# A hybrid RWKV-7 / HGRN-2 step on one core: value tiles turned in 32x32 blocks by VectorE and put in place by the stores

## The chip, the cores and the metric

The kernel runs on one core of one Trainium2 chip. The time is device microseconds of one launch. The kernel before took 1773.77 us (median of 3 runs, 1771.31 to 1775.47). PE is TensorE, PEld its weight load, DVE VectorE, ACT ScalarE, POOL GpSimd and SP SyncE, whose queue only issues transfers.

## The reference

One layer of a diffusion backbone, all in float32, over 1024 latent tokens and 128 context tokens (T = 1152). Cut to what matters here:

```python
u = h @ w_in                                   # h = modulated rmsnorm(x), [T, 1024]
q, i, zf, zb, g = split(u[:, :2560], 5)        # HGRN-2: 4 heads x 128; i are its inputs (values)
o_a = hgrn2_scan(silu(q), 1 - f, heads(i), log f) in both directions, rmsnorm, * silu(g)
r, k, v, ... = split(dwconv1d(u[:, 2560:]))    # RWKV-7: 8 heads x 64; v are its values
S = S * w_t - (S kk)(kk a) + v_t k_t;  y_t = S r_t          # in both directions
bonus = sum(r * k * r_k) * v
x = x + gate1 * (concat(o_a, o_b) @ w_out)
x = x + gate2 * ((gelu(dwconv2d(h2 @ w_gate) + b) * (h2 @ w_up)) @ w_down)
```

The projections of `w_in` come out with channels on partitions and tokens along the free axis. Two of the results are needed the other way round, tokens on partitions: the RWKV-7 values `v` (the recurrence and the bonus read them by token) and the HGRN-2 inputs `i` (right-hand side of the products over tokens).

## The kernel before

The program runs in these stages, which overlap: modulation and norm of the input; projections of `w_in` (768 groups of three fp32r matmuls of 128x128 by 384 columns, L1070 to L1072, from a high and a low part of each operand) with the RWKV-7 features of four channel pairs (`features`, from L1309) and a 32x32 elimination per pair (`elim`); the RWKV-7 recurrence (`chains`, 18 steps of 64 tokens in two groups of heads), interleaved with the HGRN-2 blocks (`hgrn_block`, `hgrn_out`); the output projection; the feed-forward part (22 blocks of channels, L2065, seven products of a Strassen-like scheme); and its down projection (L2229).

What is turned. For each pair `p` and block `tb` of 384 tokens, `features` takes `v[:, c]` [128 channels, 384 tokens] for the forward direction and a reversed copy `vs` (by POOL or ACT, L1349) for the backward one. TensorE turns each in three 128x128 transposes against `ident` into PSUM (L1353), ACT or DVE copies the result to `vt` (L1355, two buffers), and one or two transfers store it in the DRAM tensor `d_v` (`vx`), tokens as rows, in pieces of 128 floats (L1359). `hgrn_in` does the same for the part "i" of each head: copy out of PSUM (L1234), three transposes (L1238), copy (L1239), one store to `d_hv` (L1240), which holds [128, 9, 128]: for each partition the nine 128-token tiles in a row. `d_v` is loaded by `load_values` (L1703) into `X`, which POOL or ACT copies once more (L1704), and by `bonus_rows`; `d_hv` by `hgrn_block` (L1550) and `hgrn_out` (L1650).

What sets the order. The program is first recorded as some 9,600 operations. Three tables then fix everything: `SEQUENCE` is the order in which operations are issued, and so the order of each engine's own instructions; `ENGINE_OF` has a letter (V, A, G, S for DVE, ACT, POOL, SP) for each operation that could go to more than one engine, among them all copies written with `copy` and all stores written with `st` (POOL or SP); `PLACE_OF` names the buffer of each tile. Each engine works strictly in its own order and waits where an operand isn't there. Nothing is decided at run time.

Of the kernel before, what the change touches and what calls it, by code (L numbers as in the profile page):

```python
# [493 lines left out]
class Plan:  # L494


    HELPERS = ("mm", "st", "copy", "combine", "split", "load_w", "record", "either", "acc", "fetch")
    ENGINES = ("PE", "DVE", "ACT", "POOL", "SP")
    LETTER = {"V": "DVE", "A": "ACT", "G": "POOL", "S": "SP"}
    BITS = 23  # L500
# [1899 lines left out]
```

## Time and profile before

| | us |
|---|---|
| median of 3 runs | 1773.77 |
| profiled execution, whole | 1778.03 |
| its span, first to last instruction | 1776.3 |
| PE busy | 1711.1 |
| DVE busy | 1424.9 |
| ACT busy | 949.4 |
| POOL busy (transfers that it issues not counted) | 354.6 |

The span in stages, from the profile's stretches: start 0 to 44 us; projections and features to about 488 us; recurrence and HGRN-2 blocks to about 933 us; output projection to 1037 us; feed-forward part to about 1520 us; down projection to the end. How to read it: "busy" on PE includes the time in which small matmuls drain, so 96% is not peak arithmetic, but it is the share of the span in which TensorE was not waiting. A row of a group gives operation, output and input names, shape and count, then busy us and mean ns of one, then the idle time just before it and who ended that.

### The profile page before, as it was taken

How to read it: one execution, taken by the hardware profiler on the slowest of the kernel's cores; microseconds unless marked ns; L12 is line 12 of the kernel's file. 1: busy time of each engine (PE TensorE's matmuls, PEld its weight loads, DVE VectorE, ACT ScalarE, POOL GpSimd, SP SyncE). 2: the span in 40 equal slices, each digit the busy share in tenths (PEclk: the TensorE clock that was granted, in tenths of full speed). 3: DMA queues.
4: the chain of work that ended last, by engine and by line, in shares of the span. 5: the costliest groups of instructions: out<-in, count | busy, mean ns of one | idle time of the engine just before them, and what ended most of it. 6: DMA issues, size and time to landing. Idle time of an engine off the chain costs nothing.

```text
span 1776.3 us, 44618 instructions
## 1 busy us (share of the span) xinstructions
PE 1711.1 (96%) x17726; PEld 1544.9 (87%) x17726; DVE 1424.9 (80%) x2722; ACT 949.4 (53%) x1977; POOL 354.6 (20%) x546
## 2 busy tenths in 40 slices
PE   6999999999999989999999999999999999999998
PEld 4888888889988888887877889999999999888886
DVE  6548988988787878786767888898888888979765
ACT  6655766662266655564645664444444444665542
POOL 2003133153311011112210013323333322000000
PEclk8999999999999999999989999999999999999999
DMA  9326456486676678889987657877877777898683
GB/s 308 98 86 163 109 136 154 120 227 208 183 225 196 203 214 277 275 279 265 312 245 271 224 120 146 176 152 160 170 156 153 158 158 157 274 316 275 196 273 130
DMA packets 341838, 352.97 MB, mean 199 GB/s; under 512 B 69817, under 2 KB 264398, under 8 KB 341278
## 3 DMA queue, kind: packets, MB, share of 16 engines
q1 hardware_dynamic: 287518, 284.85, 52.9%
q0 software_dynamic: 54112, 65.27, 19.2%
q8 instruction: 139, 2.28, 0.5%
q14 instruction: 69, 0.57, 0.1%
HBM read 254.99 MB, written 118.10 MB: 210 GB/s over the span
## 4 chain that ended last, share of the span: by engine, by line
PE 73%; DVE 4%; DMA 4%; ACT 3%; issue 1%; POOL 1%; SPq 0%; DVEq 0%; ACTq 0%; POOLq 0%
PE banks L2065 27%; PE banks L2229 14%; PE banks L1070 4%; PE banks L1072 4%; PE banks L1071 4%; PE banks L1713 2%; PE banks L1955 1%; PE banks L1957 1%; PE banks L1956 1%; PE banks L1582 1%; PE banks L1784 1%; PE banks L1627 1%; PE banks L1760 1%; PE banks L1767 1%; PE banks L1786 1%
## 5 line engine op out<-in xcount | busy, mean ns | idle before, releaser
L1070 PE MATMUL banks<-hh,wh 128*128 128x384 f32 x768 | 278.2, 362 | 0.6 <-DVE fx L1250 0.6
L1072 PE MATMUL banks<-hh,wl 128*128 128x384 f32 x768 | 258.7, 337 | 0.0
L1071 PE MATMUL banks<-hl,wh 128*128 128x384 f32 x768 | 258.4, 336 | 0.0
L2153 DVE SCALAR_TENSOR_TENSOR low<-low,pf 128x1024 f32<-128x1024 f32 x176 | 225.7, 1282 | 10.6 <-ACT low L2147 8.0
L2065 PE MATMUL banks<-qm,wh 128*128 128x320 f32 x968 | 223.4, 310 | 0.2 <-ACT wh L2035 0.2
L2065 PE MATMUL banks<-hbm,wh 128*128 128x256 f32 x880 | 162.9, 282 | 1.5 <-ACT low L1935 1.5
L2065 PE MATMUL banks<-qm,wl 128*128 128x320 f32 x528 | 162.8, 308 | 0.2 <-DVE wl L2035 0.2
L2065 PEld LDWEIGHTS banks<-qm,wh 128*128 128x128 f32 x968 | 161.0, 189 | 0.6 <-ACT wh L2035 0.5
L1070 PEld LDWEIGHTS banks<-hh,wh 128*128 128x128 f32 x768 | 144.8, 188 | 15.7 <-issue 9.3
L1071 PEld LDWEIGHTS banks<-hl,wh 128*128 128x128 f32 x768 | 145.2, 189 | 2.7 <-issue 1.2
L1072 PEld LDWEIGHTS banks<-hh,wl 128*128 128x128 f32 x768 | 144.9, 189 | 0.0
L2065 PEld LDWEIGHTS banks<-hbm,wh 128*128 128x128 f32 x880 | 139.3, 190 | 1.8 <-ACT low L1935 1.7
L2065 PE MATMUL banks<-ham,wh 128*128 128x256 f32 (+1 forms) x616 | 131.7, 294 | 0.0
L2065 PE MATMUL banks<-hbm,wl 128*128 128x256 f32 x440 | 124.4, 283 | 0.0
L2102 ACT COPY fx<-banks 128x256 f32<-128x256 f32 (+1 forms) x132 | 52.0, 397 | 110.2 <-PE banks L2065 98.2
L2065 PEld LDWEIGHTS banks<-ham,wh 128*128 128x128 f32 x616 | 101.4, 190 | 0.3
L2065 PEld LDWEIGHTS banks<-qm,wl 128*128 128x128 f32 x528 | 99.1, 188 | 0.4 <-DVE wl L2035 0.4
L2035 ACT CAST wh<-low 128x512 fp32r<-128x512 f32 x82 | 50.5, 618 | 69.4 <-PE banks L2065 60.5
L2065 PEld LDWEIGHTS banks<-hbm,wl 128*128 128x128 f32 x440 | 84.0, 191 | 0.0
L2065 PE MATMUL banks<-ham,wl 128*128 128x256 f32 (+1 forms) x264 | 77.0, 292 | 0.0
L2035 DVE TENSOR_TENSOR wl<-low,wh 128x512 fp32r<-128x512 f32 x82 | 56.2, 689 | 22.8 <-ACT wh L2035 20.7
L2035 ACT CAST wh<-wr 128x512 fp32r<-128x512 f32 x72 | 44.6, 622 | 54.3 <-PE banks L2065 43.8
(586 smaller groups left out, 4368.2 us busy)
## 6 DMA issues: line engine op xcount, KB each, us to landing
wr<-in_w_in_dram SPq DMA_DIRECT2D x34, 512.0 KB
d_t<-in_ffn_w_down_dram POOLq DMA_DIRECT2D x60, 256.0 KB, 6.5
low<-d_a SPq DMA_DIRECT2D x54, 256.0 KB
low<-d_ak SPq DMA_DIRECT2D x64, 192.0 KB
low<-d_kb SPq DMA_DIRECT2D x36, 256.0 KB
d_a<-low POOLq DMA_DIRECT2D x16, 576.0 KB, 4.7
top<-in_ada_w_dram SPq DMA_DIRECT2D x17, 512.0 KB
low<-in_ada_w_dram SPq DMA_DIRECT2D x32, 256.0 KB
```

The source lines that it names most:

```text
L1070: mm(o, wh[:, kt, :], hh[:, kt, c], kt == 0, False)
L1071: mm(o, wh[:, kt, :], hl[:, kt, c], False, False)
L1072: mm(o, wl[:, kt, :], hh[:, kt, c], False, kt == KT - 1)
L1582: mm(pv[r, i, :], xs[:, t0:t0 + 32], view(qy, t0, [[2 * m, 16 // m], [B + m, 2], [1, m]]), True, True)
L1627: mm(ps[:, i * P:(i + 1) * P], kt[:, i * P:(i + 1) * P], val[:, i, :], True, True)
L1713: mm(pa[h][:, P * w:P * w + P], kb[hc[h], w, :], W[hc[h], A0[h] + 192 * w:A0[h] + 192 * w + P], True, True)
L1760: mm(R[hc[h], 64 * w:64 * w + 64], av(h, w, 0), X[h][:, 0, w], True, True)
L2035: split(*w, src)
L2065: pe.matmul(o, a[:, kt, :], b[:, kt, :], start=start and first, stop=last, skip_group_check=not start)
L2102: act.copy(keep[n], y[:, 0:w])
L2153: dve.scalar_tensor_tensor(av, shifted(dy, dx), tap(3 * dy + dx), av, MUL, ADD)
L2229: pe.matmul(o, x, y, start=fresh and f, stop=l, skip_group_check=not fresh)
```

## The change

The value tiles are no longer turned by TensorE. A DVE transpose turns each 32x32 block of the [128, 384] tile within its place: partition 32a + i, column 32b + j becomes partition 32a + j, column 32b + i. Partition quadrant `a` then still holds channels 32a to 32a + 31, now along the columns of each block, and tokens of the block on partitions. The new `turned_store` sends four transfers, one per quadrant, which put the block of 32 tokens and 32 channels at its rows and columns; a piece is 32 floats, 128 bytes. `d_hv` becomes [T, 128], tokens as rows, so its two loads take three pieces of 512 bytes per partition where they took one of 1536 bytes. The copy out of PSUM in `hgrn_in` is ACT's alone now. PSUM tiles and their second copies go away.

```diff
-    hvd = [dram(f"d_hv{h}", [P, NT, P]) for h in range(4)]
+    hvd = [dram(f"d_hv{h}", [T, P]) for h in range(4)]
...
-                    copy(ta, ps)
-                    pv = pbank()
-                    with plan.together():
-                        for j in range(3):
-                            pe.transpose(pv[:, j * P:(j + 1) * P], ta[:, j * P:(j + 1) * P], ident)
-                    copy(tb_, pv[:, 0:384])
-                    st(hvd[h][:, 3 * tb:3 * tb + 3, :], tb_.rearrange("p (a b) -> p a b", b=P))
+                    act.copy(ta, ps)
+                    dve.transpose(tb_, ta)
+                    turned_store(hvd[h][tb * 384:(tb + 1) * 384], tb_, 0)
...
+    def turned_store(rows, blocks, at):
+
+        n = rows.shape[0] // 32
+        for a in range(4):
+            st(rows[:, 32 * a:32 * a + 32].rearrange("(b i) c -> i b c", i=32),
+               blocks[32 * a:32 * a + 32, 32 * at:32 * (at + n)].rearrange("p (b c) -> p b c", c=32))
 ...
-                ps = pbank("sp")
-                with plan.together():
-                    for j in range(3):
-                        pe.transpose(ps[:, j * P:(j + 1) * P], vs[:, j * P:(j + 1) * P], ident)
                 vt = tl("vt", [P, 384])
-                copy(vt, ps[:, 0:384])
+                dve.transpose(vt, vs)
                 for ch, n0, n in steps_of(d, 6 * (2 - tb if d else tb), 6):
-                    at = (ch - 6 * (2 - tb if d else tb)) // 2
+                    at = 2 * (ch - 6 * (2 - tb if d else tb))
                     w0 = P * (2 * (p % 2) + d)
-                    st(vx[p // 2][64 * n0:64 * (n0 + n), w0:w0 + P].rearrange("(a p) c -> p a c", p=P),
-                       vt.rearrange("p (a b) -> p a b", b=P)[:, at:at + n // 2, :])
+                    turned_store(vx[p // 2][64 * n0:64 * (n0 + n), w0:w0 + P], vt, at)
 ...
-        ld(val, hvd[h][:, 3 * tb:3 * tb + 3, :])
+        ld(val, hvd[h][c].rearrange("(a p) e -> p a e", p=P))
 ...
 SEQUENCE = [int(i) for i in """
-1 2 17 6 18 19 0 12 13 14 15 7 11 177 184 10 27 28 4 3 20 21 29 30 33 22 24 16 34 26 31 32
+228 229 11 1 0 12 13 14 27 8 17 18 2 28 19 4 3 15 29 30 20 21 31 16 33 39 22 24 25 32 81 26
```

The three tables are new as a whole, so the order moves on every engine, also where the code is the same. In counts: 108 matmuls fewer on PE, 36 STREAM_TRANSPOSE more on DVE, 18 + 11 copies fewer on ACT; the transfers that store `d_v` go from 32 to 128, those of `d_hv` from 12 to 48; POOL issues 487 transfers in place of 357, SP 1187 in place of 1185. Of the 72 copies of values in the recurrence POOL now has 40 for 45, and of those of L1769 DVE has 6 for 15. TensorE's order keeps its large shape: the projections, features and steps of the recurrence stand at nearly the same counts of each other.

TensorE in the first block of values (L1343 is the bonus product and L1364 the decay projections; in the new program the lines are L1350 and L1366, and the projections L1074 to L1076). Before:

```order
L1072 MATMUL banks<-hh,wl_136 128x384
L1343 MATMUL banks<-hsum,top 128x2 x3
L1353 MATMUL banks<-c_ident,low 128x128 x3
L1353 MATMUL banks<-c_ident,top 128x128 x3
L1070 MATMUL banks<-hh,wh_133 128x384
```

Now:

```order
L1076 MATMUL banks<-hh,wl_136 128x384
L1350 MATMUL banks<-hsum,top 128x2 x3
L1074 MATMUL banks<-hh,wh_134 128x384
L1075 MATMUL banks<-hl,wh_134 128x384
L1076 MATMUL banks<-hh,wl_136 128x384
```

The six transposes of the two directions are gone, and projections follow at once.

DVE at the same place in the new program (L1283 the convolution's taps, L1268 the low part of a weight, L1331 to L1343 the first features; in brackets what a row waits for):

```order
L1283 SCALAR_TENSOR_TENSOR low<-low,pt 128x1024
L1358 STREAM_TRANSPOSE top<-low 128x384 [waits DVE_49]
L1358 STREAM_TRANSPOSE top<-top 128x384 [waits Activation_49]
L1268 TENSOR_TENSOR wl_136<-wr,wh_134 128x1024 [waits DMAHW3_49,PE_49,Activation_49]
L1358 STREAM_TRANSPOSE top<-low 128x384 [waits DMAHW6_49,DMASW3_49,DMAHW7_49,DMASW2_49,DVE_49]
L1358 STREAM_TRANSPOSE top<-top 128x384 [waits DMAHW1_49,DMAHW0_49,DMAHW5_49,DMASW4_49,Pool_49]
L1331 SCALAR_TENSOR_TENSOR top<-low,pt,top 128x1152 [waits Activation_49]
```

Before, no transpose of values stood on DVE. The third and fourth wait for the four transfers each of the first and second (DMAHW are SP's, DMASW POOL's), because `vt` has two buffers. The first features stand behind them.

POOL at the start of the recurrence (L1704, now L1706, the copy of values; L1820, now L1822, a store of outputs; L1798, now L1800, the decay of the state; L1613, now L1615, a small copy of the HGRN-2 blocks). Before:

```order
L1704 COPY low<-low 64x256 [waits DMAHW1_49,PE_49]
L1704 COPY low<-low 64x256 [waits DMAHW6_49,Pool_49]
L1704 COPY low<-low 64x256 [waits DMAHW2_49,PE_49]
L1613 COPY gres<-top 128x2x3 [waits DVE_49,Pool_49]
L1820 DMA d_y<-top 128x256 [waits DMASW5_49,Activation_49]
L1798 TENSOR_TENSOR low<-low,dcs 128x256 [waits DVE_49]
L1704 COPY low<-low 64x256 [waits DMAHW3_49,PE_49,Pool_49]
```

Now:

```order
L1706 COPY low<-low 64x256 [waits DMAHW5_49,PE_49]
L1800 TENSOR_TENSOR top<-top,dcs 128x256 [waits DVE_49,Pool_49]
L1800 TENSOR_TENSOR low<-low,dcs 128x256 [waits DVE_49,Activation_49]
L1822 DMA d_y<-top 128x256 [waits DMASW7_49,Activation_49]
L1615 COPY gres<-top 128x2x3 [waits DVE_49]
L1633 DMA d_hu_111<-fx 128x384 [waits DMASW0_49]
L1706 COPY low<-low 64x256 [waits DMAHW3_49,PE_49,Pool_49]
L1822 DMA d_y<-top 128x256 [waits DMASW1_49,Activation_49]
L1248 DMA d_hf_98<-fx 128x384 [waits DMASW2_49,Activation_49]
L1706 COPY low<-low 64x256 [waits DMAHW5_49,PE_49]
```

More stores stand between the copies: 103 transfers between POOL's first and last copy of values, where there were 44; SP's list between its first and last load of values is 551 rows long, where it was 603.

More of the change, by code (lines that the diff above doesn't have):

```diff
@@ new lines @@
+    "VAVAVVVAVVAAAAAAAAVVVVVASSSSGSSSSGGGGGSSGSGVVAVAVAAAAAAVVAAVVVAAVVVAVAAVAVVVAVAAGASASVSVSASVSAGVSVVGSSSASSGGVVAAGGGGVAAAGSSGAASSGSGSSSSVVAVSGSSVAAAGSG"
+    "GAASSSGSGGSGSSGSGSGSAAAAAAVSGSSSGSSVAAAAAASGGSGGGSSSSASAGASAAAAAAAASGGSSGSGGGGSSSGGSGGGSSGGAAGSSSAGSGSAAAVSGGSAAAAGGSSVASGSSASSGGVAAVSSSGAAAASSGSVASSS"
+    "SGSSGASGGGGGSSVAAAAAASGSGSSSSVAVAAAASGSGSGSSGSSASAGASAAAAAAAVGSSSGGSSGSSGGGSSSSGSGGSSAASSSSGGSSSVAAAGSGSAAAVGSGSAAGGSSGSGSGAAAASSSSVAVASSGGVAGSSSSSGSA"
+    "SGGGSSGSVAAAAAASGGSSSGSVAAAAVASGGGGGGGSGSGSGAAAAAAAASGGGSSGSGSGSSGGGSGGSSSSSAASGGSAGSSSAVAAGGSGAAAAGSGSVAGSGSGSSGGVAAASSSSAAAASSSGVAGGSSGGGSAGSGGGGSSA"
@@ L494 @@
 class Plan:
-    HELPERS = ("mm", "st", "copy", "combine", "split", "load_w", "record", "either", "acc", "fetch")
+    HELPERS = ("mm", "st", "copy", "combine", "split", "load_w", "record", "either", "turned_store", "acc", "fetch")
     ENGINES = ("PE", "DVE", "ACT", "POOL", "SP")
@@ L1649, in hgrn_out @@
             ld(sc, hsd[h][:, 3 * tb:3 * tb + 3, :])
-            ld(val, hvd[h][:, 3 * tb:3 * tb + 3, :])
+            ld(val, hvd[h][c].rearrange("(a p) e -> p a e", p=P))
             ld(g2, hqg[h][:, c])
```

51 lines of the change are left out of this document (24 added, 27 removed), and 603 rows, old and new, of the table SEQUENCE.

## The prediction

> **What bounds the kernel now.** I read the page first (busy shares and slices), then busy time by stretch, the waits of TensorE, and the groups and the chain at the lines that the change touches.
>
> ```profile
> PE 1711.1 (96%) x17726; PEld 1544.9 (87%) x17726; DVE 1424.9 (80%) x2722; ACT 949.4 (53%) x1977; POOL 354.6 (20%) x546
> PE   6999999999999989999999999999999999999998
> ...
> 0.00:44.00 44.00, 30.39 (x220) 20.92 (x220) 28.40 (x85) 30.29 (x63) 9.52 (x29) 0.88 0.94 307
> ...
> 89.00:488.00 399.00, 393.30 (x4270) 354.34 (x4269) 323.27 (x653) 223.93 (x452) 115.18 (x214) 1.00 0.58 154
> 488.00:933.00 445.00, 411.91 (x7636) 360.68 (x7636) 345.54 (x833) 253.97 (x592) 74.19 (x135) 0.98 0.83 249
> ...
> 1300.00:1500.00 200.00, 200.00 (x1504) 200.00 (x1504) 173.27 (x253) 88.24 (x171) 62.17 (x64) 1.00 0.76 154
> ```
>
> In the stretch rows the numbers are the length, then busy time of PE, weight load, DVE, ACT and POOL, the clock, the DMA share and GB/s. TensorE sets the time: it stands 65 us in 1776.3, of which 13.6 us are the loading at the start (DMA share 0.94), 5.7 lie in 89 to 488 us (projections and RWKV features), 33.1 in 488 to 933 (the recurrence), none in 1300 to 1500 (the feed-forward part). Before 488 us, work taken off TensorE should come off the span almost one for one. The 33 us are spread thinly:
>
> ```profile
> PE banks L1713 <- DMA low<-d_ak: 5.8, 4, 2.5
> PE banks L1767 <- ACT low L1762: 3.2, 3, 1.6
> PE banks L1775 <- DVE top L1611: 2.5, 1, 2.5
> ...
> PE banks L1238 <- ACT fx L1234: 1.1, 2, 0.6
> ```
>
> (us in total, times, longest.)
>
> **The change, part by part.** *Removed from TensorE:* 108 transposes, 72 at L1353 and 36 at L1238.
>
> ```profile
> L1238 PE MATMUL banks<-c_ident,fx 128*128 128x128 f32 x36 | 6.6, 291 | 1.1 <-ACT fx L1234 1.1
> L1353 PE MATMUL banks<-c_ident,low 128*128 128x128 f32 x36 | 6.3, 284 | 0.0
> L1353 PE MATMUL banks<-c_ident,top 128*128 128x128 f32 x36 | 6.2, 282 | 0.0
> ...
> 266.02 0.87 PE banks L1353 x6
> 343.48 0.80 PE banks L1353 x6
> ...
> 123.54 0.53 PE L1353 MATMUL banks<-c_ident,low 128*128 128x128 f32 x3
> 123.94 0.55 PE L1353 MATMUL banks<-c_ident,top 128*128 128x128 f32 x3
> 124.24 0.42 PE L1070 MATMUL banks<-hh,wh 128*128 128x384 f32 x1
> ```
>
> Busy time says 6.6 + 6.3 + 6.2 = 19.1 us, the upper end, since overlapping ends are counted. The chain rows give 0.80 to 0.87 us for six, the timeline 0.70 us from the first of six to the next projection matmul (124.24 - 123.54): 108 x 0.117 = 12.6 us is the lower end. I take the larger chain row, 0.87 / 6 = 0.145 us each, because a switch of operand also costs the neighbour something: 15.7 us, 10.4 of it at L1353 and 5.2 at L1238. The wait of 1.1 us at L1238 goes with them. In the order, 99 of the 108 stand ahead of the recurrence, where TensorE is 98.6% busy.
>
> *Moved between ACT and DVE:* of the copies out of PSUM, 18 + 11 go from ACT (481 to 487 ns) and 6 + 1 from DVE; 36 block transposes come to DVE.
>
> ```profile
> L1355 ACT COPY top<-banks 128x384 f32<-128x384 f32 x18 | 8.4, 487 | 2.4 <-PE banks L1353 2.4
> L1355 DVE COPY top<-banks 128x384 f32<-128x384 f32 x6 | 3.3, 556 | 1.3 <-PE banks L1353 1.3
> L1769 DVE COPY low<-banks 64x256 f32<-64x256 f32 x15 | 6.3, 421 | 7.2 <-PE banks L1767 3.5 <-PE banks L1760 1.9 <-ACT low L1769 1.2
> L1436 DVE STREAM_TRANSPOSE top<-low 128x1024 f32<-128x1024 f32 x5 | 6.2, 1239 | 0.0
> L1447 DVE STREAM_TRANSPOSE top<-top 128x1024 f32<-128x1024 f32 x5 | 10.3, 2066 | 0.1
> ...
> 123.00:412.00 289.00, 283.87 (x3303) 251.43 (x3302) 252.38 (x520) 183.27 (x380) 90.92 (x171) 0.99 0.60 153
> ```
>
> No 128x384 block transpose is in the trace. From the contiguous 128x1024 one, 1239 x 0.375 = 465 ns; from the strided one, 2066 x 0.375 = 775 ns. The new ones are contiguous, so I take 0.50 us (the lower figure and a little for the start): 18 us on DVE, bounds 16.7 and 27.9. Against it go 7 copies (3.9 us) and, by the new table of engines, 9 of the 15 copies at L1769 (3.8 us): net 10 us. In the features stretch, 123 to 412 us, DVE goes from 252.4 to about 261 (24 x 0.50 - 3.3) while TensorE goes from 283.9 to 273.5: DVE is then 94% of what TensorE needs. It still fits, but with little room. ACT, 183 of 289 us, only gains.
>
> *Stores.* A tile of values was stored by one or two transfers with pieces of 512 B; now by four per destination with pieces of 128 B.
>
> ```profile
> L1359 SPq DMA_DIRECT2D d_v<-top x22: 360/580/1456, 125.0 to 373.6; - x22
> L1359 POOL DMA_DIRECT2D d_v<-top x10: 563/748/792, 124.9 to 412.1; - x10
> DMA to landing us min/median/max: 2.3/4.4/5.0
> ...
> q1 hardware_dynamic: 12187, 5.26, 45.3%
> ...
> q1 hardware_dynamic: 287518, 284.85, 52.9%
> ```
>
> The first q1 row is of 133 to 178 us, the second of the whole run: 0.453 x 16 x 45 / 12187 = 26.8 ns for packets of 432 B on average, 0.529 x 16 x 1776.3 / 287518 = 52.3 ns for 991 B. A line through both gives 13 ns at 128 B; no saving at all would be 27 ns. 36 tiles x 1536 packets of 128 B take 45 us of all 16 engines (93 at 27 ns) in place of 26 (13,824 packets of 512 B at 30.5 ns). Spread over 123 to 652 us, +19 us (at most +67) against a share of 0.60 stays far from full: cost 0. The value loads in the recurrence get three packets for one, at the same bytes: 24 x 384 x 30.5 / 16 = 18 us of engine time at most in place of part of it; cost 0.
>
> The Trainium skill speaks against these stores: "DMA: Bandwidth & Descriptors", Specifications, puts the minimum transfer for line rate at 512 B, with read-modify-write below. Taken as "128 B costs what 512 B costs", that is the 27 ns above, and the time would move toward the 1768 of rival C, through later landings; the two q1 rows, smaller packets being cheaper, rather contradict it.
>
> The direct cost of the stores is on DVE: `vt` has two buffers, and in the new order the third transpose stands two places behind the first pair, with one weight split between. It waits for four issues (0.58 us on SP, 0.75 on POOL, shared: some 1.5 us) and a landing of up to 5.0 us. DVE stands there some 4 us once; behind it wait `kk` and the first feature products. TensorE has projections queued ahead, so I charge 1 us. The other pairs stand 12 to 50 rows apart.
>
> *The tables.* TensorE's order keeps its shape: at every 48th projection matmul the counts of features, elimination and recurrence matmuls differ by a few. In the recurrence POOL gets 103 transfers between its first and last copy of values, against 44, and SP loses 52 rows. I charge nothing for this, and put it into the rivals.
>
> Sum: -15.7 - 1.1 + 1.0 = -15.8 us, so 1776.3 becomes 1760.5 in the span. The profiled execution took 1778.03 us, 4.3 more than the median of the runs, 1773.77; I carry the difference to the median: **1758 us**.
>
> **Rivals.** *B, more than the transposes:* fewer stores on SP let the loads of the recurrence start earlier, and the new order may close some of the 33.1 us there. For it: 5.8 us of L1713 wait on loads. Against it: the other waits there are many and short. A quarter to half of 33 us: 1742 to 1750.
>
> *C, DVE takes over in the features stretch:* 261 us of work, plus 12 value blocks with some 2 us of waiting for stores each, is 285 of the 289 us. The 10.4 us of L1353 are lost, only the 5.2 at L1238 stay: 1768. Against it: DVE's waits there are now small, and projections buffer TensorE.
>
> *D, slower: POOL's queue in the recurrence.*
>
> ```profile
> L1704 POOL COPY low<-low 64x256 f32<-64x256 f32 x45 | 25.7, 573 | 171.9 <-DMA low<-d_v 129.0 <-PE banks L1582 14.2 <-issue 10.9
> L1820 POOL DMA_DIRECT2D d_y<-top x17 | 9.5, 561 | 54.2 <-ACT top L1817 54.2
> ```
>
> POOL copies the values of each step (40 of 72 now), and every store queued ahead holds that copy by 0.56 us and by whatever the store waits for. 59 more stores x 0.56 = 33 us; if all of it reached the recurrence, 1758 + 33 = 1791. It decides from 48% (15.8 / 33) coming through. For it: POOL is strictly in order, and stores wait for ACT (54.2 us in 12 waits at L1820). Against it: POOL stood 129 us waiting for the loads of values, which these stores can use, and is busy 74 of 445 us.
>
> *E, the change frees TensorE and nothing follows:* the projections only run ahead and the recurrence, bound by its own chain, ends when it did: 1773. Against it: it starts when the work before it is done, 99 transposes sooner.
>
> **How the numbers follow.** The forecast (1750 to 1767) gets 0.48, B 0.20, C 0.15, D 0.13, E 0.04. No change means within 0.2%, 1770.2 to 1777.3. Faster: 0.48 + 0.20 + 0.10 of C = 0.78. Same: 0.05 of C, 0.03 of D, 0.03 of E = 0.11. Slower: the rest, 0.11. The range runs from the low end of B, 1741, to 1778, the part of D that gives back only a little more than the gain; outside lie about 0.03 of B and 0.11 of D.
>
> **What would show it.** Right: TensorE busy about 1692 to 1696 us with some 65 us of standing; 89 to 488 us of today done by about 475, with the first L1713-like matmuls 12 to 15 us earlier; DVE rows of STREAM_TRANSPOSE 128x384 near 0.5 us; the feed-forward part as long as now. C shows as TensorE waiting on DVE products in the features stretch and DVE above 93% there; D as POOL rows of stores ahead of value copies and TensorE waiting for POOL at L1775-like lines; B as less than 25 us of standing in the recurrence. I am wrong if the recurrence or the feed-forward part grows by more than 5 us, or if a transpose on DVE takes 0.78 us.

## The result, and the profile after

The changed kernel takes 1785.64 us (median of 7 runs, 1781.56 to 1794.51), the kernel before on the same chip 1774.65 us (7 runs, 1771.31 to 1778.84): a ratio of 1.0070, 95% interval 1.0047 to 1.0092. It is slower by 0.7%, some 12 us, where 1758 us was forecast. The profiled execution of the changed kernel took 1789.6 us, 4.0 above its median; that of before stood 4.3 above its own, so the two traces can be compared directly. Spans of single executions of one kernel differ by several us, so no difference below some 5 us between two traces is explained here by the traces alone. Medians here and below leave out three slow executions (2329 us of no_turning, 2965 and 5946 us of the kernel before).

The page's busy times after:

```profile
PE 1707.3 (95%) x17618; PEld 1538.5 (86%) x17618; DVE 1441.9 (81%) x2733; ACT 935.5 (52%) x1966; POOL 421.8 (24%) x672
```

All 108 transposes are gone (17726 to 17618), yet PE's busy time fell by 3.8 us only, to 1707.3 where 1692 to 1696 was forecast, and it stands 80.5 us in place of 65.2. Where, is seen when the span is cut at the same points of TensorE's work in both kernels: the first and the 1584th of the 2304 projection matmuls, the first and the last matmul of the gate and up projections (L2065, L2067 after), and the end. Up to the 1584th, the two kernels have the same projection, feature and elimination matmuls; the kernel before has 90 transposes more. Busy time by stretch; columns as in the prediction. Before:

```profile
70.00:454.50 384.50, 378.80 (x4036) 338.41 (x4035) 306.82 (x611) 223.77 (x451) 106.01 (x196) 1.00 0.56 150
454.50:1024.40 569.90, 535.47 (x8501) 467.53 (x8500) 441.52 (x1019) 321.72 (x739) 88.91 (x160) 0.99 0.80 244
1024.40:1535.70 511.30, 508.34 (x3769) 504.54 (x3769) 446.06 (x654) 239.82 (x465) 146.87 (x151) 1.00 0.76 160
1535.70:1776.30 240.60, 232.06 (x1035) 189.30 (x1033) 183.86 (x306) 115.10 (x223) 2.44 (x3) 0.99 0.74 243
```

After:

```profile
72.20:465.40 393.20, 374.75 (x3947) 333.71 (x3947) 319.24 (x637) 211.28 (x434) 144.61 (x265) 0.98 0.59 141
465.40:1031.10 565.70, 534.57 (x8484) 464.99 (x8483) 446.76 (x1020) 321.09 (x744) 124.89 (x231) 0.99 0.82 249
1031.10:1540.30 509.20, 504.27 (x3746) 501.40 (x3745) 444.44 (x648) 235.95 (x460) 141.84 (x142) 1.00 0.75 158
1540.30:1787.80 247.50, 237.90 (x1058) 193.61 (x1057) 187.39 (x311) 118.01 (x228) 3.88 (x5) 0.99 0.74 240
```

The 11.5 us are 2.2 at the start (72.2 against 70.0), 8.7 in the features stretch, -4.2 from there to the end of the recurrence and the output projection, -2.1 in the gate and up projections and 6.9 from there to the end. So the features stretch, from which the gain should have come, is where most was lost. The first L1713 matmul of the recurrence (L1715 after), forecast 12 to 15 us earlier, came 2.5 us later, at 486.3 against 483.8. It isn't at the same place in the two orders: 1728 projection matmuls start before it in the kernel before and 1683 in the changed one, so the new order put 45 of them behind the start of the recurrence: some 8 us of work, estimated from the 0.17 us from one to the next at 344.4 to 345.9 us of the changed kernel. Cut there, the features stretch looks as long as before (414.1 against 413.8 us), but holds less work. That TensorE's order keeps its counts, as is said ahead of the prediction and in it, is right up to the 1584th projection and not at this point.

In the features stretch TensorE's clock was at half for 3.4 us before and for 17.1 us after (the granted clock in the seventh column):

```profile
288.80:292.20 3.40, 3.40 (x49) 2.96 (x52) 3.04 (x6) 2.12 (x5) 0.91 (x2) 0.50 0.60 159
```

```profile
293.50:307.20 13.70, 11.72 (x144) 9.82 (x145) 7.48 (x13) 5.02 (x13) 4.32 (x9) 0.50 0.60 128
413.00:416.40 3.40, 0.71 (x4) 0.39 (x3) 3.33 (x6) 0.49 (x1) 2.36 (x6) 1.00 0.56 187
416.40:419.80 3.40, 3.40 (x12) 3.40 (x12) 3.16 (x10) 0.00 (x0) 3.40 (x7) 0.50 0.96 268
```

Half of the busy time in such pieces is lost: 1.7 us before, (11.72 + 3.40) / 2 = 7.6 after. That gives a balance that is used for the runs below, work at full clock + standing + half clock lost. Up to the 1584th projection it is 377.1 + 5.7 + 1.7 = 384.5 before and 367.2 + 18.4 + 7.6 = 393.2 after: TensorE was spared 9.9 us of work, but stood 12.7 us longer and lost 5.9 us more to the half clock. Up to the first L1713 matmul it is 406.4 + 5.7 + 1.7 = 413.8 before; the runs under the old tables, where TensorE's order is that of before, are compared with this.

What TensorE waited for in 89 to 488 us after, where before no wait was over 1.1 us:

```profile
PE banks L1466 <- issue: 4.1, 2, 3.3
PE banks L1074 <- DVE fx L1250: 2.7, 1, 2.7
PE banks L1399 <- DVE top L1391: 2.3, 1, 2.3
PE banks L1350 <- DVE top L1346: 2.3, 1, 2.3
PE banks L1074 <- ACT low L1275: 1.5, 1, 1.5
PE banks L1074 <- ACT low L1277: 1.5, 1, 1.5
PE banks L1399 <- ACT low L1409: 1.2, 1, 1.2
PE banks L1074 <- ACT low L1279: 1.1, 1, 1.1
```

None of these names a block transpose or a store of values. The transposes themselves, with what DVE waited for ahead of them:

```profile
L1358 DVE STREAM_TRANSPOSE top<-low 128x384 f32<-128x384 f32 x12 | 6.9, 574 | 2.8 <-DMA d_v<-top 2.7
L1358 DVE STREAM_TRANSPOSE top<-top 128x384 f32<-128x384 f32 x12 | 6.9, 572 | 0.5 <-DMA d_v<-top 0.4
L1239 DVE STREAM_TRANSPOSE fx<-fx 128x384 f32<-128x384 f32 x12 | 6.8, 570 | 1.9 <-ACT fx L1238 1.8
```

### The profile page after: what moved, and what is told of

The parts are those of the page before. It is cut to its first block, busy times and chain, and to the rows that moved or that the text cites. A ratio compares the mean times of both kernels' runs of the same rounds, so it can differ in the third digit from the quotient of the medians.

```text
span 1787.8 us, 44540 instructions
## 1 busy us (share of the span) xinstructions
PE 1707.3 (95%) x17618; PEld 1538.5 (86%) x17618; DVE 1441.9 (81%) x2733; ACT 935.5 (52%) x1966; POOL 421.8 (24%) x672
## 5 line engine op out<-in xcount | busy, mean ns | idle before, releaser
L1074 PE MATMUL banks<-hh,wh 128*128 128x384 f32 x768 | 281.1, 366 | 9.1 <-DVE fx L1250 4.8
L1076 PE MATMUL banks<-hh,wl 128*128 128x384 f32 x768 | 260.4, 339 | 0.0
L2067 PE MATMUL banks<-qm,wh 128*128 128x320 f32 x968 | 224.6, 311 | 0.0
L1074 PEld LDWEIGHTS banks<-hh,wh 128*128 128x128 f32 x768 | 146.3, 190 | 29.7 <-issue 10.6
L2067 PE MATMUL banks<-hbm,wh 128*128 128x256 f32 x880 | 162.8, 282 | 2.1 <-ACT fx L2104 2.1
L2067 PE MATMUL banks<-qm,wl 128*128 128x320 f32 x528 | 163.3, 309 | 0.2 <-DVE wl L2037 0.2
L2067 PEld LDWEIGHTS banks<-qm,wh 128*128 128x128 f32 x968 | 161.6, 190 | 0.1
L1076 PEld LDWEIGHTS banks<-hh,wl 128*128 128x128 f32 x768 | 146.0, 190 | 0.0
L2067 PEld LDWEIGHTS banks<-hbm,wh 128*128 128x128 f32 x880 | 139.2, 190 | 2.4 <-ACT fx L2104 2.4
L2067 PE MATMUL banks<-ham,wh 128*128 128x256 f32 (+1 forms) x616 | 132.3, 294 | 0.3 <-DVE ham L1997 0.3
L2067 PE MATMUL banks<-hbm,wl 128*128 128x256 f32 x440 | 124.4, 283 | 0.0
L2067 PEld LDWEIGHTS banks<-ham,wh 128*128 128x128 f32 x616 | 101.6, 189 | 1.0 <-DVE ham L1997 0.5
L2067 PEld LDWEIGHTS banks<-qm,wl 128*128 128x128 f32 x528 | 99.5, 189 | 0.5 <-DVE wl L2037 0.5
L2067 PEld LDWEIGHTS banks<-hbm,wl 128*128 128x128 f32 x440 | 83.9, 191 | 0.0
L2175 POOL DMA_DIRECT2D d_t<-in_ffn_w_down_dram x44 | 50.7, 1254 | 117.1 <-DMA d_t<-d_t 86.7
L2067 PE MATMUL banks<-ham,wl 128*128 128x256 f32 (+1 forms) x264 | 77.0, 292 | 0.0
```

The lines of the kernel that those rows point to most:

```text
L1074: mm(o, wh[:, kt, :], hh[:, kt, c], kt == 0, False)
L1076: mm(o, wl[:, kt, :], hh[:, kt, c], False, kt == KT - 1)
L2067: pe.matmul(o, a[:, kt, :], b[:, kt, :], start=start and first, stop=last, skip_group_check=not start)
L2175: acc(td[j][k], b)
```

## The experiments

The order, the engines and the buffers stand in three tables, so the edit and the tables can be run apart: the old tables were carried over to other code, operation by operation, with new operations put where those that they replace had stood. "Old tables" below means this. The median is of 4 to 12 executions; the ratio is to the kernel before on the same chip (7 to 23 executions, median 1772.9 to 1774.7 us), so the ratios are the safer comparison between rows.

| run | code, tables | us | ratio, 95% interval |
|---|---|---|---|
| changed kernel | changed, new | 1785.6 | 1.0070 (1.0047 to 1.0092) |
| edit_old_tables | changed, old | 1795.6 | 1.0111 (1.0093 to 1.0129) |
| hg_old_tables | HGRN-2 inputs alone, old | 1784.2 | 1.0064 (1.0043 to 1.0086) |
| rw_old_tables | RWKV values alone, old | 1791.9 | 1.0091 (1.0075 to 1.0107) |
| no_turning | no turning, old | 1765.8 | 0.9953 (0.9937 to 0.9969) |
| dve_old_stores | DVE turns, one store, old | 1774.8 | 0.9997 (0.9981 to 1.0014) |
| four_stores | TensorE turns, four stores, old | 1790.2 | 1.0090 (1.0069 to 1.0110) |
| quarter_stores | TensorE turns, four stores of 512 B pieces, old | 1786.2 | 1.0072 (1.0049 to 1.0094) |
| edit_dve_relief | changed, old, 51 operations to ACT | 1806.1 | 1.0174 (1.0150 to 1.0197) |
| edit_spread | changed, old, stores spread | 1809.9 | 1.0216 (1.0190 to 1.0242) |
| edit_pool | changed, old, stores on POOL | 1795.4 | 1.0121 (1.0096 to 1.0147) |
| after_start | changed, new, start loads moved | 1787.5 | 1.0078 (1.0055 to 1.0100) |
| after_old_stores | DVE turns, one store, new | 1783.6 | 1.0052 (1.0033 to 1.0070) |
| after_small_turns | changed, small turns, new | 1786.4 | 1.0070 (1.0049 to 1.0092) |
| old_code_new_tables | before, new | 1804.3 | 1.0175 (1.0156 to 1.0193) |
| after_old_tail | changed, new, old from the recurrence's end | 1779.5 | 1.0031 (1.0011 to 1.0050) |
| edit_filled | edit_old_tables with fillers | 1795.1 | 1.0119 (1.0099 to 1.0140) |
| after_tail_filled | after_old_tail with fillers | 1777.2 | 1.0016 (1.0002 to 1.0029) |
| before_filled | before with fillers | 1775.7 | 1.0013 (0.9998 to 1.0027) |

### The edit apart from the tables

The code of the change, whole or by halves, under the old tables; and the changed kernel with two loads of the start moved.

> The changed code (all 36 value tiles turned by VectorE, four stores where one stood) in the order, on the engines and in the buffers of the kernel before: each block transpose stands where the copy out of PSUM stood, its stores where and on the queue where the old store stood; five transposes stand 1 to 15 places earlier, because the buffer they read is taken by the next tile. Theory 1, the new tables cost the time and the edit itself gains: TensorE is spared the 12.6 us by which its busy time of the projection and features stretch fell in the changed kernel, so about 1762 us (1757 to 1768). Theory 2, the edit itself costs it, because VectorE and the store queues feed the features later: 1775 to 1790 us, with TensorE standing at least 12 us more than before between 89 and 488 us.

> Only the 12 HGRN input tiles are turned by VectorE, in the order, on the engines and in the buffers of the kernel before; the RWKV values stay on TensorE. Theory 1 (tables): a third of the gain, 4 to 5 us, about 1770 us. Theory 2 (the edit): no gain, 1773 to 1778 us. If this one gains and the one with the RWKV values alone does not, the features stretch is where VectorE cannot take the work.

> Only the 24 RWKV value tiles are turned by VectorE, in the order, on the engines and in the buffers of the kernel before; the HGRN inputs stay on TensorE. Theory 1 (tables): two thirds of the gain, 8 to 10 us, about 1765 us. Theory 2 (the edit): 1774 to 1786 us, with TensorE waiting for VectorE and ACT products in the features stretch.

> The changed kernel with two loads of the start moved: the identity matrix first, and the first projection weight (512 KB, first in the changed kernel) after the first activations, where the kernel before has it. If the 7.3 us for which TensorE waits on the identity are what makes the first projections 2.3 us late, and the lateness is carried to the end: about 1783 us. If what follows absorbs it: 1785 to 1786 us as the changed kernel.

Theory 1, that the tables alone cost the time, fell: under the old tables the edit costs 1.1%, more than in the changed kernel, and each half alone costs too. All three runs came out slower than the ranges of both theories. The loss is nearly all in the features stretch, here up to the first recurrence matmul, 17.8 of 19.8 us in the trace (edit_old_tables):

```profile
70.30:501.90 431.60, 412.03 (x4219) 368.03 (x4217) 336.10 (x671) 221.92 (x443) 123.30 (x237) 0.95 0.59 145
```

By the balance: 392.5 us of work (13.9 less than before), 19.6 standing (13.9 more), 19.6 lost to the half clock (17.9 more). From the end of the recurrence on, this kernel's stages are as long as those of before. TensorE's wait of 7.3 us for the identity is no cause in the changed kernel: with the identity first (after_start) it went, one of 3.9 us on VectorE stood there instead, as in the kernel before, and the time stayed. But the first projection came no earlier either (73.8 us against 72.2), so what an earlier start would be worth was not tested.

### Transposes or stores

Two factors under the old tables: who turns, and how the tile is stored.

```diff
 no_turning:
-                pe.transpose(ps[...], vs[...], ident)   (three)
-                copy(vt, ps[:, 0:384])
+                copy(vt, vs)
 dve_old_stores:
-                turned_store(...)
+                st(vx[...].rearrange("(a p) c -> p a c", p=P), vt.rearrange("p (a b) -> p a b", b=P)[...])
 four_stores: the transposes and copies of before, then
+                turned_store(...)
 edit_dve_relief: 51 letters V of ENGINE_OF in the features and the elimination become A
```

> The kernel before without any turning: the 108 transposes on TensorE are gone, and each copy out of PSUM, on the same engine as before, is a copy from the tile that would have been turned; the stores stay as they were. It leaves the transposition of the 36 value tiles out. Theory P, TensorE bounds the features stretch, as my forecast had it: 12.6 to 15 us off, 1760 to 1763 us. Theory V, VectorE's queue sets the pace there as much as TensorE: TensorE's work falls by 13 us, its standing grows by nearly as much, and the time stays within 6 us of the kernel before, 1769 to 1775 us.

> VectorE turns all 36 tiles in 32x32 blocks, but each tile is stored by the one or two transfers of the kernel before (pieces of 512 B), in its order, on its engines and in its buffers; so the values land in blocks at wrong places, and the permuting of blocks is what it leaves out. Theory V, the transposes on VectorE cost the time: 1790 to 1797 us, as with the four stores. Theory S, the four stores with 128 B pieces cost it, through the queues that issue them or late landings: 1760 to 1770 us.

> TensorE turns all tiles as in the kernel before, and copies bring them out of PSUM as before; only the stores are the four of the changed kernel, with pieces of 128 B, on the queue of the old one. The values then land at wrong places, since the blocks are permuted twice. Theory S: 1785 to 1795 us. Theory V: 1773 to 1778 us.

> The changed code in the order and buffers of the kernel before, as in the first experiment (1795.6 us), but 51 operations of the RWKV features and the elimination that VectorE had from the table of engines go to ACT: some 20 us off VectorE, against the 16.7 us net that the block transposes brought. Theory V: at least 15 us faster than the first experiment, 1765 to 1780 us. Theory S, or ACT's queue being as tight as VectorE's: 1790 us or more.

| | stores as before | four stores |
|---|---|---|
| TensorE turns | 1774.4 (the kernel before) | 1790.2 |
| VectorE turns | 1774.8 | 1795.6 |

Theory V, which I held after the first runs because the stretch grew with what VectorE was given (7.5, 11.9 and 17.8 us for 12, 24 and 36 tiles), fell here as the price of the edit: the stores cost 16 us without any turning on VectorE. Taking 15 us off VectorE in the stretch (336.1 to 321.3) by giving them to ACT made it slower by another 10 us, so ACT is no better place for that work. And no_turning gives a ceiling: with all turning left out the time falls by 0.5%, 8 to 9 us, between the ranges of theories P and V. The 15.8 us of the forecast were not to be had under these tables. What was to be had came nearly one for one: up to the first recurrence matmul TensorE's work fell by 9.0 us, its standing rose by 2.1, the half clock lost fell by 1.7, and the stretch was 8.6 us shorter (405.2 against 413.8). (The trace of that run is 14.3 us shorter in the span, its median 8.6 us.)

VectorE's turning isn't free, though. With the old stores it brings the time back to that of the kernel before (1774.8, in neither theory's range), and the intervals of no_turning and dve_old_stores lie apart: it takes back the whole 8 to 9 us that leaving out the turning gives. The features stretch shows it, up to the 1584th projection, no_turning and then dve_old_stores:

```profile
69.50:446.10 376.60, 368.79 (x3948) 328.44 (x3947) 304.55 (x611) 223.82 (x451) 103.93 (x196) 1.00 0.57 153
```

```profile
69.80:455.10 385.30, 374.57 (x3948) 333.38 (x3947) 315.31 (x631) 214.69 (x429) 101.44 (x196) 0.98 0.56 149
```

By the balance, 368.8 + 7.8 + 0.0 = 376.6 and 366.1 + 10.7 + 8.5 = 385.3: with VectorE turning, TensorE stands 2.9 us more and loses 8.5 us to the half clock. (VectorE also takes over the place of copies that ACT had; the two aren't told apart.)

How four stores cost 16 us is seen at one place, SP's queue at 366 us. Before (start, us, row):

```profile
365.92 0.43 SPq L1359 DMA_DIRECT2D d_v<-top  x1
366.45 0.47 SPq L1420 DMA_DIRECT2D d_ak<-top  x1
...
372.56 1.80 SPq L1359 DMA_DIRECT2D d_v<-top  x2
374.45 0.47 SPq L1420 DMA_DIRECT2D d_ak<-top  x1
```

four_stores:

```profile
366.96 5.56 SPq L1371 DMA_DIRECT2D d_v<-top  x8
372.62 0.46 SPq L1431 DMA_DIRECT2D d_ak<-top  x1
374.19 2.95 SPq L1245 DMA_DIRECT2D d_hv<-fx  x4
...
379.97 5.50 SPq L1371 DMA_DIRECT2D d_v<-top  x8
385.56 0.40 SPq L1431 DMA_DIRECT2D d_ak<-top  x1
```

Eight issues hold the queue for 5.56 us, and the store of `d_ak` behind them goes out 6 us late, the next one 11 us late. VectorE may not write its next product into that store's source (`kr`, two buffers) until it has landed, and TensorE stands behind VectorE. The largest waits of VectorE and of TensorE in four_stores in 366 to 400 us:

```profile
DVE top L1399 <- DMA d_ak<-top: 6.2, 1, 6.2
...
PE banks L1408 <- DVE low L1424: 4.2, 1, 4.2
```

Before, VectorE waited there for no transfer, and TensorE 0.5 us. 11.8 of the 16 us are lost between the 384th and the 432nd group of three projection matmuls, 359 to 396 us of before.

### Count or size of the stores, and other places for them

```diff
 quarter_stores (before, and):
-                    st(vx[...] , vt...[:, at:at + n // 2, :])
+                    for a in range(0, P, 32):
+                        st(vx[...][a:a + 32], vt...[a:a + 32, at:at + n // 2, :])
 edit_spread: SEQUENCE with the value stores one at a time behind other rows of their queue, letters S G S G
 edit_pool: all 176 letters of the value stores G
 after_old_stores: dve_old_stores under the new tables
```

> The kernel before, with TensorE turning all tiles, its tables and its pieces of 512 B; only each store of a value tile is cut into four, one for each 32 partitions, on the queue of the old one. Nothing else changes, and nothing is left out. Theory Q, it is the number of issues on an in-order queue that costs (eight in a row held SP for 5.6 us in the trace of the run with four stores, and the store of d_ak behind them went out at 372.6 us in place of 366.5): as with the four stores of 128 B pieces, 1784 to 1793 us. Theory B, it is the small pieces: 1773 to 1778 us.

> The changed code in the order and buffers of the kernel before, as in the first experiment (1795.6 us), but of each four stores two go to SP and two to POOL, and on each queue one of them goes out behind each other instruction of that queue, so that no eight stand in a row; 29 of the 176 must go earlier because their buffer is wanted. Theory Q: at least 10 us faster than the first experiment, 1770 to 1786 us. Theory B: 1790 us or more.

> The changed code in the order and buffers of the kernel before, with all 176 value stores on POOL (48 in the first experiment came there by the old letters or fewer). Theory Q with SP as the queue that matters: 1772 to 1785 us. If POOL's queue matters as much, since VectorE's scans wait for memsets and the d_akp and d_kb stores stand there too (an issue on POOL took 0.55 to 0.6 us): 1788 to 1805 us.

> The changed kernel with its own tables, VectorE turning all tiles, but one or two stores for each tile with pieces of 512 B as before, at the place of the first of the four; the permuting of blocks is left out, so the values land at wrong places. If the stores are what costs in the changed kernel as they do under the old tables (20.8 us there): 1763 to 1773 us. If its tables have hidden them and the loss is the start, the recurrence and VectorE: 1780 to 1787 us.

The count it is, for the most part: with pieces of 512 B and nothing else changed, four issues for one cost 0.7%, 12 us, by the same chain (SP's queue, then VectorE's and TensorE's waits):

```profile
366.46 3.90 SPq L1366 DMA_DIRECT2D d_v<-top  x8
370.46 0.38 SPq L1427 DMA_DIRECT2D d_ak<-top  x1
...
DVE top L1395 <- DMA d_ak<-top: 5.8, 1, 5.8
...
PE banks L1404 <- DVE low L1420: 5.4, 1, 5.4
```

That 128 B pieces cost anything more (1790.2 against 1786.2) is not shown, the intervals overlap. My two cures failed: edit_spread, for which theory Q had said 1770 to 1786 us, took 1809.9, and edit_pool 1795.4, the time of edit_old_tables. In the traces, stores held back on their queues keep `vt` full, and VectorE's transposes wait for them, 23.3 us in nine waits; stores moved to POOL hold the memsets there that VectorE's scans need. edit_spread, then edit_pool:

```profile
DVE top L1358 <- DMA d_v<-top: 23.3, 9, 4.2
```

```profile
DVE top L1384 <- POOL top L1377: 7.2, 2, 5.3
```

The last run, after_old_stores, turned the question. Under its own tables the changed kernel gains 2 us by having one store for four, within the intervals (by the ratios 3 us, and anything from -2 to 8). So the stores cost little or nothing there; that the new tables had made room for them is the likely reason, and not tested.

### The tables

```diff
 old_code_new_tables: the code of before; transposes and copy where the block transpose stands, in two other PSUM banks
 after_small_turns (the changed kernel, and):
-                dve.transpose(vt, vs)
+                dve.transpose(vt[:, 0:w_], vs[:, 0:w_])     (w_ 384 or 32)
 after_old_tail: SEQUENCE, ENGINE_OF and PLACE_OF of before from the end of the recurrence on
```

> TensorE turns all tiles and one or two stores put each away, as in the kernel before, but in the order, on the engines and in the buffers of the changed kernel; the three transposes stand where the block transpose stood, their copy right behind, in two other PSUM banks. Nothing is left out. Theory T, the new tables cost time whatever turns the values: 1781 to 1792 us. Theory E, under the new tables too it is the edit that costs: 1768 to 1776 us.

> The changed kernel, its tables, stores and waits, but of 24 of the 36 tiles VectorE turns only the first 32 columns of 384 (the rest of those tiles is what the buffer held, which leaves that part of the turning out). That takes some 9 us off VectorE (24 times 0.57 us less about 0.2). Theory E with VectorE's time as what TensorE waits for: 1774 to 1780 us. If VectorE's time is not it: 1783 to 1787 us.

> The changed kernel up to the end of the recurrence, and from there (the output projection, the feed-forward part, the down projection: code that the change doesn't touch) the order, engines and buffers of the kernel before. The trace has these stages 5.1 us longer in the changed kernel (509.2 + 240.8 against 511.3 + 233.7 us). If that is the new table's doing: 1779 to 1782 us. If it is the state in which the recurrence leaves the queues: 1784 to 1787 us.

| | old tables | new tables |
|---|---|---|
| code of before | 1772.9 (the kernel before) | 1804.3 |
| changed code | 1795.6 | 1785.6 |

Each code is better under its own tables, the old one by 31 us, the changed one by 10 (7 by the ratios). Under the new tables the edit gains 18.7 us (1804.3 to 1785.6), but those tables start 31 us behind, more than theory T had said (1781 to 1792 us). A caution: in both crossed runs I put the exchanged operations where their counterparts stood, and no table was made anew for them, so part of the 31 us may be the crossing.

That stalls of the changed kernel belong to its order shows in the waits of old_code_new_tables in the same stretch (89 to 488 us). Six of the eight waits shown above for the changed kernel stand here too, on the same instructions and nearly as long, though TensorE does the turning (L1070 here is L1074 there, L1343 is L1350, L1397 is L1399):

```profile
PE banks L1070 <- DVE fx L1250: 2.7, 2, 2.5
...
PE banks L1343 <- DVE top L1339: 1.8, 2, 1.5
...
PE banks L1070 <- ACT low L1277: 1.5, 1, 1.5
PE banks L1070 <- ACT low L1275: 1.3, 1, 1.3
...
PE banks L1397 <- ACT low L1407: 1.2, 1, 1.2
PE banks L1070 <- ACT low L1279: 1.1, 1, 1.1
```

They are projection matmuls that wait for a PSUM bank to be emptied, and feature products that wait for VectorE: places at which the order has TensorE ahead of ACT and VectorE. The delay is in every trace under the new tables. The 1584th projection matmul starts at 454.5 us in the kernel before (453.6 in before_filled, 455.1 in dve_old_stores); at 465.4 in the changed kernel, at 459.5 to 467.8 in the five variants of it, and at 477.2 in old_code_new_tables.

VectorE's added time is not the main cause under these tables: after_small_turns turned 32 columns in 27 of the 36 tiles (the expectation said 24), which took 9.8 us off VectorE (20.6 to 10.7), and the time stayed, to within some 5 us by the intervals.

```profile
L1360 DVE STREAM_TRANSPOSE top<-low 128x32 f32<-128x32 f32 (+1 forms) x12 | 3.6, 301 | 2.6 <-DMA d_v<-top 2.5
```

Its features stretch was 4.9 us shorter in the trace up to the 1584th projection (388.3 against 393.2), and what follows up to the gate and up projections 4 us longer.

The tail is settled better. With the old order, engines and buffers from the end of the recurrence on, after_old_tail takes 1779.5 us, 6 us less than the changed kernel, as the 4.8 us by which the two last stretches differ had said:

```profile
1023.90:1535.20 511.30, 508.34 (x3770) 504.56 (x3769) 446.10 (x655) 241.31 (x466) 146.91 (x151) 1.00 0.76 161
1535.20:1775.50 240.30, 232.03 (x1034) 189.26 (x1033) 183.28 (x305) 115.33 (x222) 2.44 (x3) 0.99 0.74 242
```

Both are as long as before to within 0.3 us. So about half of the 11 us is the new tables' order of code that the change doesn't touch. (The intervals of the two ratios overlap a little; the lengths of the stretches bear the reading out.)

### Does a stall of TensorE cost twice?

In the traces many of the longer stalls are followed by a piece of 3.4 us, or a multiple, at half clock: in edit_old_tables seven of the eight of 1.5 us and more behind the start. One of them:

```profile
222.00:225.50 3.50, 1.02 (x6) 0.70 (x5) 3.31 (x9) 2.47 (x6) 0.98 (x4) 1.00 0.54 101
225.50:235.70 10.20, 10.12 (x128) 7.89 (x132) 7.24 (x14) 5.12 (x12) 0.39 (x3) 0.50 0.78 172
```

TensorE was busy for 1.02 of 3.50 us, and then ran at half clock for 10.2. Three kernels got idle matmuls into such stalls.

```diff
+    for tag_, n_ in [("ms", 6), ("ms", 8), ...]:
+        filler = tl(tag_, [P, 512])
+        with plan.together():
+            for _ in range(n_):
+                mm(filler[:, 0:128], ident, ident, True, True)
 and each such group in SEQUENCE ahead of the matmul that waits
```

> The first experiment (changed code under the old tables, 1795.6 us) with filler matmuls, identity by identity into a free PSUM bank, 3 to 14 of them (estimated 0.28 us each) ahead of five matmuls for which TensorE waited 1.0 to 4.4 us between 148 and 398 us; nothing reads the filler. In its trace TensorE's granted clock was half for 41 us of that stretch, in pieces that begin within a microsecond or so of these waits, which costs 20 us. Theory G, a stall of TensorE costs twice, once by itself and once through the half clock behind it: filling the stalls takes 8 to 15 us off, 1780 to 1788 us. If the half clock has another cause: 1795 us or, by fillers that run over, up to 1800.

> The changed kernel with the old tail (1779.5 us) and the same fillers ahead of seven matmuls for which TensorE waited 1.5 to 2.4 us (five in the features stretch, one in the recurrence, one at the start of the feed-forward part). Its features stretch had 20 us at half clock, 10 us lost. Theory G: 5 to 9 us off, 1771 to 1775 us, level with or below the kernel before. Otherwise 1779 to 1783 us.

> The kernel before with the same fillers ahead of six matmuls for which TensorE waited 1.4 to 2.5 us, five in the recurrence. There 17 us at half clock (8 us lost) lie behind such waits, but TensorE is not what the recurrence waits for most of the time. Theory G with a recurrence that can use a faster TensorE: 3 to 7 us off, 1767 to 1771 us. If the recurrence's own chain hides it: 1772 to 1776 us.

The stalls do bring half clock, though not all of it. Where they were filled much of it went: in the recurrence of before_filled none is left (488 to 1024 us, before and then filled):

```profile
488.00:1024.00 536.00, 501.57 (x8174) 435.13 (x8175) 419.60 (x973) 312.09 (x722) 79.16 (x142) 0.98 0.81 249
```

```profile
488.00:1024.00 536.00, 509.12 (x8274) 442.37 (x8273) 424.67 (x983) 315.95 (x728) 78.23 (x142) 1.00 0.83 251
```

In the features stretch of edit_filled the loss fell from 19.6 to 11.9 us. And it isn't one trace alone: the mean granted clock over all executions rose from 0.9860 to 0.9897 (edit_old_tables to edit_filled), from 0.9915 to 0.9952 (after_old_tail to after_tail_filled) and from 0.9946 to 0.9956 (before to before_filled). But the gain that theory G foresaw did not come: no kernel became faster by more than its uncertainty, and before_filled went the other way within its interval. Two readings are left. Where TensorE stands it is waiting for the chain through ACT, VectorE and the queues, and running faster behind the stall only brings it to the next wait sooner; then the half clock lost, in the balance, is partly time in which TensorE would have stood. Or the fillers ran over and took back what they gave: in edit_filled TensorE's full-clock work rose by 12.5 us, of which an estimate of 10.9 is the 39 fillers at 0.28 us. No run tells the two apart.

No version that computes the whole layer beat the kernel before; the nearest with all of the change in it, after_tail_filled at 1777.2 us, is 0.16% slower, interval 0.02% to 0.29%.

## Why the prediction was wrong

The sum was one gain of 15.7 us and, for all the rest, charges of nothing or 1 us. The step that failed is these zeros: VectorE's transposes hidden, the stores free, the new tables free. The gain itself was too large as well.

**TensorE sets the time, and before 488 us work taken off it comes off the span almost one for one.** This held as far as it goes. In no_turning, where the transposes go and nothing takes their place, 9.0 us less work made the stretch 8.6 us shorter, and the median fell by as much. In the changed kernel 9.9 us of work went up to the 1584th projection and the stretch grew by 8.7, since TensorE stood 12.7 us longer and lost 5.9 more to the half clock. Its added waits for others outweighed the work it was spared.

**15.7 us off TensorE.** As a gain this term was too large. With all 108 transposes left out, no_turning is 8 to 9 us faster (5 to 11 by the interval), below the lower end of 12.6 us. For the 90 transposes ahead of the 1584th projection, 13.1 us at 0.145 us each, the balance gives 8.3 us in no_turning and 9.9 in the changed kernel, and more only where TensorE stands more (13.3 us in edit_old_tables). The larger chain row had been taken for what a switch of operand costs the neighbour; no run shows that cost by itself.

**VectorE's block transposes, 0.50 us, 18 us in all, hidden.** 0.57 us and 20.6 us, and VectorE's busy time rose by 17.0 us where net 10 was forecast. (By the prediction's own figures VectorE has 95% of what TensorE needs, 261 of 273.5 us, not 94%.) Hidden failed under the old tables: dve_old_stores gives back all of the 8 to 9 us that no_turning gains. Under the new ones after_small_turns shows no cost, to within some 5 us.

**The tables, charged nothing.** I compared the counts of matmuls at every 48th projection and found the shape kept; what a table sets is also at which instruction one engine meets another, which such counts don't show. The new tables cost 6 us in the tail, shown by after_old_tail. In the features they bring stalls of their own, shown by the same waits with the old code and by the late 1584th projection in every trace under them. That the 8.7 us lost there are the tables' alone is argued: stores and VectorE's time are each bounded only to some 5 to 8 us there. Whether a table made anew for this edit could avoid it wasn't tried.

**Stores, charged nothing.** I costed the packets on the DMA engines, and that was right: their share went from 0.56 to 0.59 in the features stretch, and 128 B pieces showed no cost beyond the interval. The queue that issues them was the missing term: 132 issues more, 0.5 to 0.75 us each where they stand in a row on SP. I had weighed it for POOL in the recurrence (rival D) but not for SP in the features, where a store of `d_ak` stands behind. Under the old tables four stores cost 16 us with TensorE turning and 21 with VectorE turning, the whole loss of the edit; in the changed kernel, 2 us that aren't apart from nothing. The Trainium skill's rule on small transfers ("DMA: Bandwidth & Descriptors", Specifications), weighed in the forecast, would have had the 512 B pieces of quarter_stores spare the cost; they spared 4 us of 16, which isn't apart from nothing.

**The wait at the third and fourth value transpose, 4 us once, charged 1.** Two waits, 3.1 us in all; right, and small.

**The rivals.** D, the one on the slower side, had the wrong place: from the 1584th projection to the gate and up projections the changed kernel is 4.2 us shorter, and with all value stores on POOL (edit_pool) the time is that of edit_old_tables. B, with less than 25 us of standing in the recurrence, did not occur (31.1 us of standing from the 1584th projection to the gate and up projections, 34.4 before). C, VectorE taking over in the features, is what dve_old_stores shows under the old tables, and there all of the gain went, not only that of L1353; for the changed kernel it isn't shown. None of the rivals had VectorE, the SP queue and the order together outweigh the gain, nor a stage without a changed line lose 6 us through its table. Slower had been given 0.11.

## What to carry to other kernels

Where tables or a planner have brought the engines into step, the engine that is 99% busy is not for that the only bound: leave the work out altogether first (no_turning), and take what that gains as the ceiling, then add back one by one what takes its place. Cut two traces where the same work is done (here the 1584th projection), not at the first instruction of the next stage, which another order can move. Count the issues on each in-order queue, not only bytes and packets, and look at what stands behind them and which buffer waits for that. And a change that brings new tables is two changes: run the new code under the old tables and the old code under the new before anything is said of either.

## What the runs showed of the hardware that was not expected

TensorE's half clock can follow short stalls. A stall of 2.6 us in a stretch of 3.5 was enough for 10.2 us at half clock, one of 2.7 us (413.0 to 416.4 in the changed kernel, busy 0.71 of 3.40) for 3.4 us. The Trainium skill ("TensorE: Matmul & The Clock Gate", Part 1) tells of a free-running window of 3.4 us after which an idle TensorE falls to half; the pieces of 3.4 us and multiples agree, but here a window that was 20 to 30% busy sufficed, not only an idle one. The busy share of one such stretch doesn't decide it either: in the changed kernel 344.8 to 348.2 us (busy 1.48 of 3.40) was followed by no half clock and 290.1 to 293.5 (2.07 of 3.40) by 13.7 us of it, and in the kernel before the piece at 288.8 follows 3.4 us in which TensorE was busy for 3.31. What decides stays open.

SP took little longer to issue a store of up to 384 pieces of 128 B than one of up to 96 pieces of 512 B, by the median; the eight in a row at 366 us took 5.56 against 3.90 us. The issues of four_stores and of quarter_stores, with their shortest, median and longest time in ns:

```profile
L1371 SPq DMA_DIRECT2D d_v<-top x88: 303/476/2037, 124.8 to 385.0; - x88
```

```profile
L1366 SPq DMA_DIRECT2D d_v<-top x88: 303/428/1964, 124.4 to 382.8; - x88
```

A block transpose of 128x32 took some 0.21 us, (3.6 - 3 x 0.57) / 9 from the row of after_small_turns, in which 3 of the 12 are whole, against 0.57 us for one of 128x384 with twelve times the columns.
